# A two-layer hybrid decoder: a plain last eighth of the last layer's MLP, the loads of the DRAM sum on GpSimd's queue, decay two heads at a time, and mixing norms as columns

## The chip, the cores and the metric

The kernel runs on one core of one Trainium2 chip. The core has TensorE (PE; its weight loads appear as PEld), VectorE (DVE), ScalarE (ACT), GpSimd (POOL) and SyncE (SP), which only issues DMAs here. Time is the device time of one execution in microseconds; the median of three runs before is 1518.3 us (1516.29 to 1518.72).

## The reference

T is 512 tokens, D is 1024, and there are two layers. What the change touches is set off below by comments.

```python
def hybrid_layer(x, g_mix, w_in, sinks, w_a, w_b, w_out, g_mlp, w_up, w_down):
    h = rmsnorm(x, g_mix)                    # the mixing norm
    aq, ak, av, rq, rk, rv, rg, ga, gb = jnp.split(h @ w_in, SPLIT_POINTS, axis=-1)
    ya = sliding_window_sink_attention(rope_half(aq), rope_half(ak), av, sinks) @ w_a
    r = chunkwise_retention(retention_rotation(rq), retention_rotation(rk) * 128**-0.5, rv)   # four heads, decay
    r = r * lax.rsqrt(jnp.mean(r * r, axis=-1, keepdims=True) + EPS)
    yb = (r * jax.nn.silu(rg)) @ w_b
    x = x + (jax.nn.sigmoid(ga) * ya + jax.nn.sigmoid(gb) * yb) @ w_out
    h2 = rmsnorm(x, g_mlp)
    return x + jnp.square(jax.nn.relu(h2 @ w_up)) @ w_down      # D_FF = 4096, in eight blocks of 512
# after both layers: rmsnorm(x, g_final)
```

## The kernel before

**Products.** Activations lie transposed: 128 features on the partitions, tokens along a row. Every float32 operand is cut into a high part (ACT copies it to float32r, L301, L354) and a low part (DVE subtracts, L302, L355), and each product is three matmuls, high by high, high by low and low by high (`products`, L347 to L349).

**Weights.** They come in units of 128 x 1024 float32 (512 KB), in the order that `unit_order` lists. `load_until` issues their loads on SP's queue into five `raw` buffers, up to `AHEAD` = 4 units ahead of the split; `split_until` cuts them `SPLIT` = 3 units ahead of the matmuls. The instructions are put in order on each engine by a planner that simulates the program; an engine then executes its queue strictly in that order, and so does SP with its DMAs. The planner takes a DMA early if its buffer is free.

**The mixing stage.** `group` multiplies the first four units into four PSUM banks; its argument `meanwhile` names work to do after unit 0, 1, 2 or 3. In layer 1 this is `carried` after unit 0 (it finishes the x of layer 0, scales it, and sums its squares in `acc`, L477), `prepare` after unit 2 and `stats` after unit 3. `Rms.prepare` splits `acc`; `Rms.finish`, called by `stats`, multiplies both parts by a matrix of ones (L489), which gives every partition the sum over features of each token, and takes the root (ACT, L490) and the reciprocal (DVE, L491) of the 128 x 512 result. `scaled_tables` multiplies the rotary tables by it, and `rotate` (L537 to L543) uses those tables to empty the banks of k and q. `rstd_columns` turns the same norm into one column for each block of 128 tokens (four transposes). Attention and `retention` run as generators in the background of the products.

**Decay.** `Head.scores` multiplies the scores of a retention head by its decay tile `dm` (L851). Each head loads its own 256 KB tile (L841) on SP's queue into the one buffer of tag `acc`, which the squares of the norm use too. Tiles of 128 x 1024 float32 (`big`) share six buffers: the rotary tables, the gates `z` and `gb`, attention's `whole`, retention's `rr`, and in the MLP `z`, `xg`, `sums` and `y`.

**The MLP.** It runs over eight blocks e of 512 hidden features. `pair` multiplies twice 256 hidden features and `down` multiplies 512 by 1024 of `w_down`, both by a scheme with seven products of half-size blocks in place of eight; `Forms` makes the sums of activations that it wants. The sums of weights are made in DRAM by DMAs on POOL's queue, which add as they write (`sum_steps`, L213 to L227), five steps for every nine calls of `pace` in the mixing stage; `load_part` and `load_block` read them back. In a `down`, a unit feeds 2 x 2 x 3 = 12 matmuls of 512 columns, and seven units make 84. For e below 7 the results are added into a DRAM tensor `y` by adding DMAs on POOL's queue (`Adding`, L1219). For e = 7, `Ending` loads the four 512 KB parts of `y` back on SP's queue (L1233) when the block begins, and DVE adds the last results to them (L1248). In layer 1 they land in `x`, and the final norm and the output follow for each block of 128 tokens (L1256 to L1268).

Of the kernel before, what the change touches and what calls it, by code (L numbers as in the profile page):

```python
# [55 lines left out]
def unit_order():  # L56
# [9 lines left out]
    for e in range(N_BLOCK):  # L66
        if e == 0:
            order += [("w_up", u) for u in range(4)]
        else:
            order += [("pair", 2 * e - 2 + i, part) for i in range(2) for part in range(4)]  # L70
        order += [("block", e, part) for part in range(7)]
# [40 lines left out]
def decoder(ctx, tc, xT, x_first, w_in, w_a, w_b, w_out, w_up, w_pair, w_down, tables, decay, band, g_last, out):  # L112
# [45 lines left out]
    order = [(layer, *u) for layer in range(DEPTH) for u in unit_order()]  # L158
# [17 lines left out]
    def load_until(n):  # L176
        while state["loaded"] < min(n, len(order)):
# [6 lines left out]
            else:  # L184
                raws[i] = raw_tile()
                for at in halves(i):
                    queue = nc.scalar if i == 0 and at.start == 0 else nc.sync
                    queue.dma_start(raws[i][:, at], weights[name][layer, j][:, at])
# [11 lines left out]
    sums_last = [dram.tile([P, 2 * UNIT], F32, name=f"sums_last{l}") for l in range(DEPTH)]  # L200

    def sum_steps(layer):

        jobs = []
        for e in range(N_BLOCK):
            if e:
                jobs += [(sums_up[layer][n], w_pair[layer, n], UNIT) for n in (2 * e - 2, 2 * e - 1)]
            jobs.append((sums_down[layer][e], w_down[layer, e], 2 * UNIT))
        last = None
        for job in jobs + [None]:  # L210
# [6 lines left out]
            last = job  # L217
            yield
        e = N_BLOCK - 1
        both = sums_last[layer].rearrange("p (a n) -> p a n", a=2)  # L220
        first = sums_down[layer][e][:, UNIT:].unsqueeze(1).broadcast_to([P, 2, UNIT])
        r11, r12 = (w_down[layer, e][:, a * UNIT : (a + 1) * UNIT] for a in (0, 3))
        nc.gpsimd.dma_start(both, r11.unsqueeze(1).broadcast_to([P, 2, UNIT]))
        yield
        nc.gpsimd.dma_start(both, first, accum_op=ALU.add)
        yield
        nc.gpsimd.dma_start(both[:, 1, :], r12, accum_op=ALU.add)  # L227
# [4 lines left out]
    def pace(src):  # L232

        pace_count[0] += 1
        if steps and pace_count[0] * 5 // 9 > (pace_count[0] - 1) * 5 // 9:
# [27 lines left out]
    def load_block(i):  # L263
        layer, _, e, part = order[i]
        if part in (2, 4) and e < N_BLOCK - 1:
            return
        raws[i] = raw = raw_tile()
        source, at = {
            0: (w_down[layer, e], 0),
            1: (sums_down[layer][e], 1),  # L270
            2: (sums_last[layer], 0),
            3: (w_down[layer, e], 3),
            4: (sums_last[layer], 1),
# [210 lines left out]

    def inverse_rms(both, n, dest):
# [18 lines left out]
    class Rms:  # L504
# [15 lines left out]
    def layer_body(layer):  # L520
# [36 lines left out]
        rcol = small.tile([P, NB], F32, tag="rcol", name="rcol", bufs=2)  # L557

# [7 lines left out]

        def stats_first():
            rms_mix.prepare()
            stats()

        def rstd_columns():

            ps = bank(ps_aux, "rcol")
            for b in range(NB):
                nc.tensor.transpose(ps[:, b * P : (b + 1) * P], rstd()[:, b * P : (b + 1) * P], ident)
            nc.scalar.activation(rcol, ps.rearrange("p (b q) -> p b q", q=P)[:, :, 0], AF.Copy)

# [40 lines left out]
        def put_q(c):  # L618
# [18 lines left out]
            {0: squares, 1: stats_first} if layer == 0 else {0: carried.pop(), 2: rms_mix.prepare, 3: stats},  # L637
# [144 lines left out]
        def values(pair):  # L782
# [48 lines left out]
        class Head:  # L831
# [62 lines left out]

        def retention(pair):
# [31 lines left out]
        rstd_columns()  # L927
# [5 lines left out]
        qk(1)  # L933

# [105 lines left out]
        def column_factors():  # L1040
            ps = bank(ps_aux, "ssq")
            acc = acc_of.pop(g_mlp)
            for b in range(NB):
# [457 lines left out]
```

## Time and profile before

| | before |
|---|---|
| median of three runs | 1518.3 us |
| the profiled execution's own time | 1520.31 us |
| its span, first to last instruction | 1518.4 us |
| PE busy | 1477.2 us (97%) |
| DVE busy | 1059.8 us (70%) |
| ACT busy | 945.6 us (62%) |
| POOL busy | 239.6 us (16%) |
| mean granted TensorE clock | 0.987 of full speed |
| moved by DMA | 292.55 MB, 193 GB/s |

A line of the timeline gives the start in us from the beginning of the span, the length in us, the engine, the line of the kernel, the operation, the tile written and the tiles read, and the shape; "[4.48 <-DVE s L851]" says that the engine was idle for 4.48 us before it and that an instruction of DVE on L851 ended the wait. SPq and ACTq are the queues on which those engines issue DMAs. A line of the stages gives a stretch, its length, the busy time and number of instructions of each engine, the granted PE clock (1.00 is full speed), the share of the 16 DMA engines' time and the rate in GB/s. A line of the chain of waits gives start, length and what the chain passed through.

### The profile page before, as it was taken

Reading aid. Unit: us, or ns where it says so; the run is one execution under the profiler, and the core shown is the slowest. Engines: PE = TensorE matmul, PEld = TensorE weight load, DVE = VectorE, ACT = ScalarE, POOL = GpSimd, SP = SyncE. Lnnn points to the kernel's source line nnn. Section 1 sums busy time; section 2 is a strip of 40 time slices with the busy share of each in tenths; the row PEclk is TensorE's granted clock in tenths of the full one; section 3 lists DMA queues with packets and bytes.
Section 4 is the critical chain, followed back from the end, with each engine's and each line's share of the span. In section 5 each row is a group of like instructions: output and inputs, shape, how many; then the busy total and the mean of one; then the engine's idle time right before and its main releaser. Section 6 shows DMA issues by size and latency. Waiting matters only on the chain.

```text
span 1518.4 us, 21303 instructions
## 1 busy us (share of the span) xinstructions
PE 1477.2 (97%) x7767; PEld 1271.5 (84%) x7767; DVE 1059.8 (70%) x1602; ACT 945.6 (62%) x1560; POOL 239.6 (16%) x337
## 2 busy tenths in 40 slices
PE   9999999899999999999999999999999999999986
PEld 7888888788889899998778888878888889899975
DVE  7877667564677777775987775667547677677757
ACT  7656454443568888886655563546325788888865
POOL 0001211010002222222001011110000122222220
PEclk9999999999999999999999999999999999999998
DMA  7655997566327888889747579975643388888893
GB/s 263 194 158 159 265 285 193 159 180 165 99 74 214 211 214 218 222 212 227 253 131 206 166 193 255 262 208 156 168 136 109 109 217 218 204 214 220 219 233 118
DMA packets 103481, 292.55 MB, mean 193 GB/s; under 512 B 11856, under 2 KB 11984, under 8 KB 99280
## 3 DMA queue, kind: packets, MB, share of 16 engines
q0 software_dynamic: 38656, 114.84, 36.3%
q1 hardware_dynamic: 64000, 175.04, 34.3%
q8 instruction: 61, 1.00, 0.3%
q10 hardware_dynamic: 720, 1.31, 0.2%
q14 instruction: 44, 0.36, 0.1%
HBM read 237.66 MB, written 118.49 MB: 235 GB/s over the span
## 4 chain that ended last, share of the span: by engine, by line
PE 72%; DMA 11%; issue 7%; DVE 5%; ACT 3%; POOL 1%; SPq 0%; DVEq 0%; ACTq 0%; POOLq 0%
PE mm L347 19%; PE mm L348 19%; PE mm L349 19%; DMA raw<-w_pair_in 3%; DMA raw<-w_down_in 2%; DMA y<-y 2%; DMA dm<-decay_in 2%; DVE lo L302 2%; PE rv L347 2%; DMA y<-eu 2%; PE rv L349 2%; PE rv L348 2%; ACT hi L301 1%; PE b L347 1%; PE b L348 1%
## 5 line engine op out<-in xcount | busy, mean ns | idle before, releaser
L301 ACT ACTIVATE hi<-raw 128x1024 fp32r<-128x1024 f32 (+1 forms) x366 | 372.9, 1020 | 313.4 <-PE mm L348 192.0
L302 DVE TENSOR_TENSOR lo<-raw,hi 128x1024 fp32r<-128x1024 f32 (+1 forms) x367 | 427.9, 1170 | 188.2 <-ACT hi L301 184.1
L347 PE MATMUL mm<-xh,hi 128*128 128x512 f32 (+1 forms) x1008 | 360.0, 360 | 16.5 <-ACT eu L1129 11.6
L349 PE MATMUL mm<-xh,lo 128*128 128x512 f32 (+1 forms) x1008 | 357.3, 357 | 0.7 <-DVE lo L302 0.7
L348 PE MATMUL mm<-xl,hi 128*128 128x512 f32 (+1 forms) x1008 | 357.9, 357 | 0.0
L347 PE MATMUL mm<-r,hi 128*128 128x256 f32 (+1 forms) x736 | 239.1, 325 | 0.5 <-ACT mm L1127 0.5
L348 PE MATMUL mm<-r,hi 128*128 128x256 f32 (+1 forms) x736 | 239.3, 325 | 0.0
L349 PE MATMUL mm<-r,lo 128*128 128x256 f32 (+1 forms) x736 | 239.2, 325 | 0.0
L347 PEld LDWEIGHTS mm<-xh,hi 128*128 128x128 f32 x1008 | 192.4, 191 | 45.2 <-ACT eu L1129 13.5
L349 PEld LDWEIGHTS mm<-xh,lo 128*128 128x128 f32 x1008 | 192.0, 190 | 26.3 <-DVE lo L302 0.9
L348 PEld LDWEIGHTS mm<-xl,hi 128*128 128x128 f32 x1008 | 192.3, 191 | 25.6
L347 PEld LDWEIGHTS mm<-r,hi 128*128 128x128 f32 x736 | 140.5, 191 | 13.8 <-ACT mm L1127 0.7
L348 PEld LDWEIGHTS mm<-r,hi 128*128 128x128 f32 x736 | 140.4, 191 | 13.3
L349 PEld LDWEIGHTS mm<-r,lo 128*128 128x128 f32 x736 | 140.3, 191 | 11.3
L1219 POOL DMA_DIRECT2D y<-eu x56 | 47.3, 851 | 403.3 <-ACT eu L1217 399.2
L1219 POOL DMA_DIRECT2D y<-y x112 | 97.9, 1277 | 64.1 <-DMA y<-eu 19.9
L348 PE MATMUL mm<-lo,r 128*128 128x512 f32 x256 | 98.3, 393 | 0.0
L349 PE MATMUL mm<-hi,r 128*128 128x512 f32 x256 | 94.4, 390 | 0.0
L347 PE MATMUL mm<-hi,r 128*128 128x512 f32 x256 | 93.0, 396 | 0.2
L261 DVE TENSOR_TENSOR raw<-raw 128x512 f32<-128x512 f32 x56 | 38.5, 687 | 66.1 <-DMA raw<-sums_up 53.8
L347 PE MATMUL b<-hi,r 128*128 128x512 f32 x192 | 75.3, 392 | 1.9 <-DVE y L1248 1.4
L348 PE MATMUL b<-lo,r 128*128 128x512 f32 x192 | 74.9, 390 | 0.0
(255 smaller groups left out, 2341.1 us busy)
## 6 DMA issues: line engine op xcount, KB each, us to landing
raw<-w_in_in SPq DMA_DIRECT2D x89, 512.0 KB, 5.1
sums_down<-w_down_in POOLq DMA_DIRECT2D x32, 1024.0 KB, 11.3
y<-y POOLq DMA_DIRECT2D x120, 256.0 KB, 7.7
sums_up<-w_pair_in POOLq DMA_DIRECT2D x56, 512.0 KB, 10.5
raw<-w_down_in SPq DMA_DIRECT2D x48, 512.0 KB, 8.3
raw<-w_pair_in SPq DMA_DIRECT2D x84, 256.0 KB, 4.1
raw<-sums_down SPq DMA_DIRECT2D x32, 512.0 KB, 8.7
y<-eu POOLq DMA_DIRECT2D x58, 256.0 KB, 5.6
```

The lines of the kernel that those rows point to most:

```text
L261: nc.vector.tensor_tensor(raws[i][:, at], last[:, LEFT], last[:, RIGHT], ALU.add)
L301: nc.scalar.activation(hi[:, at], raw[:, at], AF.Copy)
L302: nc.vector.tensor_tensor(lo[:, at], raw[:, at], f32(hi[:, at]), ALU.subtract)
L347: nc.tensor.matmul(ps, ah, bh, start=start and i == 0, stop=False, **more)
L348: nc.tensor.matmul(ps, ah, bl, start=False, stop=False, **more)
L349: nc.tensor.matmul(ps, al, bh, start=False, stop=stop and i == n - 1, **more)
L1219: nc.gpsimd.dma_start(y[:, block, i * T : (i + 1) * T], t, **how)
```

## The change

1. **Plain last eighth.** In layer 1, block e = 7 multiplies `w_down` in the ordinary way: a new input `w_end` holds its 512 rows in four units of 128 x 1024 in place of the seven units of the block, and `down_plain` makes 4 units x 4 token blocks x 2 halves x 3 = 96 matmuls of 512 columns. Token blocks 0 and 1 are summed over the four units as these arrive, in four banks, and blocks 2 and 3 after them, a half at a time. The forms of this block, its DRAM sums and `sums_last` of layer 1 fall away.
2. **Loads of the DRAM sum.** The four loads of `y` in `Ending` are issued on POOL's queue.
3. **Decay.** `load_decay` loads the tiles of two heads in one DMA of 512 KB into a `big` buffer: the first pair's before `values(0)`, the second pair's after the scores of head 1.
4. **Mixing norms.** `prepare` sums `acc` over features with four matmuls by a single column of ones (`token_sums`), takes root and reciprocal of the 128 x 4 result, spreads it on the diagonals of four 128 x 128 blocks, and splits that tile; `finish` multiplies by the ones as before and copies the bank. The columns serve the retention values, and `rstd_columns` is gone. In layer 0, `prepare` follows unit 1 and `stats` unit 2; layer 1 keeps 2 and 3.
5. **Pace.** A step of the DRAM sums is taken at each second call of `pace`; a layer has 48 calls, 24 steps in layer 0 after the change (26 before) and 22 in layer 1.

```diff
@@ unit_order(layer)
+        if layer == DEPTH - 1 and e == N_BLOCK - 1:
+            order += [("w_end", k) for k in range(4)]
+        else:
+            order += [("block", e, part) for part in range(7)]
@@ load_until
+                    source = w_end[j] if name == "w_end" else weights[name][layer, j]
+                    queue.dma_start(raws[i][:, at], source[:, at])
@@ sum_steps
+            if e < whole:
+                jobs.append((sums_down[layer][e], w_down[layer, e], 2 * UNIT))
...
+        if whole == N_BLOCK:
...
+            nc.gpsimd.dma_start(sums_last, r11.unsqueeze(1).broadcast_to([P, 2, UNIT]))
             yield
+            nc.gpsimd.dma_start(sums_last, s1.unsqueeze(1).broadcast_to([P, 2, UNIT]), accum_op=ALU.add)
+            nc.gpsimd.dma_start(sums_last[:, 1, :], r12, accum_op=ALU.add)
@@ pace
-        if steps and pace_count[0] * 5 // 9 > (pace_count[0] - 1) * 5 // 9:
+        if steps and pace_count[0] % 2 == 0:
@@
+    def token_sums(acc):
+        ps = bank(ps_aux, "ssq")
+        for b in range(NB):
+            nc.tensor.matmul(ps[:, b : b + 1], acc[:, b * P : (b + 1) * P], f32(ones)[:, 0:1], start=True, stop=True)
+        return ps
@@ class Rms
         def prepare(self):
-            self.parts = sum_parts(acc_of.pop(self.which))
+            acc = acc_of.pop(self.which)
+            ps = token_sums(acc)
+            self.columns = small.tile([P, NB], F32, tag="rcol", name="rcol", bufs=2)
+            nc.scalar.activation(self.columns, ps[:, :NB], AF.Sqrt, bias=eps, scale=1.0 / D)
+            nc.vector.reciprocal(self.columns, self.columns)
+            wide = temp("wide")
+            nc.vector.tensor_tensor(
+                wide.rearrange("p (b q) -> p b q", q=P),
+                ident.unsqueeze(1).broadcast_to([P, NB, P]),
+                self.columns.unsqueeze(2).broadcast_to([P, NB, P]),
+                ALU.mult,
+            )
+            self.parts = sum_parts(wide)
         def finish(self):
             self.value = tmp.tile([P, T], F32, tag="rstd", name="rstd", bufs=1)
-            inverse_rms(self.parts, D, self.value)
+            ps = bank(ps_aux, "ssq")
+            for i, part in enumerate(self.parts):
+                nc.tensor.matmul(ps, ones, part, start=i == 0, stop=i == 1)
+            nc.scalar.activation(self.value, ps, AF.Copy)
@@ layer_body
-            {0: squares, 1: stats_first} if layer == 0 else {0: carried.pop(), 2: rms_mix.prepare, 3: stats},
+            {0: squares, 1: rms_mix.prepare, 2: stats} if layer == 0 else {0: carried.pop(), 2: rms_mix.prepare, 3: stats},
...
-                split(view(hi), view(lo), ps, rcol[:, b : b + 1])
+                split(view(hi), view(lo), ps, rms_mix.columns[:, b : b + 1])
@@ Head.scores
-                    self.dm = tmp.tile([P, T], F32, tag="acc", name="dm", bufs=1)
-                    nc.sync.dma_start(self.dm, decay[:, h, :])
+                    self.dm = decays[h // 2][:, h % 2, :]
@@
+        def load_decay(pair):
+            decays[pair] = big("dm")
+            nc.sync.dma_start(decays[pair], decay[:, 2 * pair : 2 * pair + 2, :])
@@ retention
                     head.scores(js)
+                    if pair == 0 and head is two[1] and js[0]:
+                        load_decay(1)
                     yield
@@
-        rstd_columns()
...
         qk(1)
+        load_decay(0)
         values(0)
@@ the MLP
+        def first_plain(z):
+            nc.scalar.activation(z, z, AF.Square)
+            split(*u_forms.tiles[0][0], z.rearrange("p a (b t) -> p (a b) t", t=H))
...
+        def down_plain(into):
+            sums.free()
...
+            units = []
+            early = [[bank(pool, "mm") for pool in (ps_mm, ps_aux)] for _ in range(2)]
+            for k in range(4):
+                units.append(unit("w_end", layer))
+                for m in range(2):
+                    for half in range(2):
+                        add(early[m][half], m, half, k)
+            for m in range(2):
+                for half in range(2):
+                    into.put(half, m // 2, m % 2, early[m][half], 1)
+            for m in range(2, NB):
+                for half in range(2):
+                    ps = bank(ps_mm, "mm")
+                    for k in range(4):
+                        add(ps, m, half, k)
+                    into.put(half, m // 2, m % 2, ps, 1)
@@ class Ending
-                    nc.sync.dma_start(two, y[:, 2 * j : 2 * j + 2, i * T : (i + 1) * T])
+                    nc.gpsimd.dma_start(two, y[:, 2 * j : 2 * j + 2, i * T : (i + 1) * T])
...
-                if last or i == 0:
+                if i == 0:
@@
-            down(e, into)
+            if last and e == N_BLOCK - 1:
+                down_plain(into)
+            else:
+                down(e, into)
```

More of the change, by code (lines that the diff above doesn't have):

```diff
@@ L111, in decoder @@
 @with_exitstack
-def decoder(ctx, tc, xT, x_first, w_in, w_a, w_b, w_out, w_up, w_pair, w_down, tables, decay, band, g_last, out):
+def decoder(ctx, tc, xT, x_first, w_in, w_a, w_b, w_out, w_up, w_pair, w_down, w_end, tables, decay, band, g_last, out):
     nc = tc.nc
@@ L155, in decoder @@
     spill = dram.tile([P, KD, T], F32, name="spill")
-    order = [(layer, *u) for layer in range(DEPTH) for u in unit_order()]
+    order = [(layer, *u) for layer in range(DEPTH) for u in unit_order(layer)]
     raws, parts = {}, {}
@@ L199, in decoder @@
     sums_down = [dram.tile([N_BLOCK, P, 2 * UNIT], F32, name=f"sums_down{l}") for l in range(DEPTH)]
-    sums_last = [dram.tile([P, 2 * UNIT], F32, name=f"sums_last{l}") for l in range(DEPTH)]
+    sums_last = dram.tile([P, 2, UNIT], F32, name="sums_last")
     def sum_steps(layer):
+        whole = N_BLOCK if layer < DEPTH - 1 else N_BLOCK - 1
         jobs = []
@@ L267, in load_block @@
         raws[i] = raw = raw_tile()
+        if part in (2, 4):
+            nc.sync.dma_start(raw, sums_last[:, part // 2 - 1, :])
+            return
         source, at = {
@@ L1040, in column_factors @@
         def column_factors():
-            ps = bank(ps_aux, "ssq")
-            acc = acc_of.pop(g_mlp)
-            for b in range(NB):
-                nc.tensor.matmul(ps[:, b : b + 1], acc[:, b * P : (b + 1) * P], f32(ones)[:, 0:1], start=True, stop=True)
+            ps = token_sums(acc_of.pop(g_mlp))
             nc.vector.tensor_scalar(factor, ps[:, :NB], 1.0 / D, EPS, ALU.mult, ALU.add)
@@ L1092, in second_rest @@
         def second_rest(z):
+            if not kept:
+                return
             kept.pop()
@@ L1332, in layer_body @@
             else:
+                plain = last and e == N_BLOCK - 1
                 into = Ending() if e == N_BLOCK - 1 else Adding(e)
```

46 lines of the change are left out of this document (22 added, 24 removed).

## The prediction

> **What bounds the kernel now.** I read the page's busy times first, then PE's timeline for its idle stretches, then the stages around each.
>
> ```profile
> PE 1477.2 (97%) x7767; PEld 1271.5 (84%) x7767; DVE 1059.8 (70%) x1602; ACT 945.6 (62%) x1560; POOL 239.6 (16%) x337
> ```
>
> PE is the bound: what the change can win is matmuls, PE's idle time, time at a lower clock, and the tail. The timeline of PE has five long idle stretches; the sixth row is a short one, for comparison.
>
> ```profile
> 275.37 0.47 PE L347 MATMUL ret<-r,r 128*128 128x128 f32 x1 [4.48 <-DVE s L851]
> ...
> 722.12 0.58 PE L347 MATMUL mm<-xh,hi 128*128 128x256 f32 x1 [3.56 <-ACT eu L1129]
> ...
> 784.24 0.47 PE L347 MATMUL mm<-xh,hi 128*128 128x512 f32 x1 [3.56 <-DVE rot L541]
> ...
> 1025.67 0.48 PE L347 MATMUL ret<-r,r 128*128 128x128 f32 x1 [3.96 <-DVE s L851]
> ...
> 1479.87 0.58 PE L347 MATMUL mm<-xh,hi 128*128 128x256 f32 x1 [5.29 <-ACT eu L1129]
> ```
>
> ```profile
> 746.50 0.47 PE L347 MATMUL b<-hi,r 128*128 128x512 f32 x1 [1.40 <-DVE y L1248]
> ```
>
> The stages right behind the five (PE alone: length, busy time, granted clock, DMA) show a second price of each.
>
> ```profile
> 275.37:280.27 4.90, 4.90 (x17) 0.50 0.33 65
> ...
> 722.11:727.41 5.30, 5.29 (x21) 0.50 1.04 406
> ...
> 784.24:788.85 4.61, 4.61 (x13) 0.63 0.35 117
> ...
> 1025.67:1031.20 5.53, 5.53 (x18) 0.50 0.17 47
> ...
> 1479.87:1485.17 5.30, 5.30 (x23) 0.50 0.97 381
> ```
>
> ```profile
> 745.00:750.00 5.00, 3.60 (x20) 3.03 (x20) 5.00 (x8) 0.53 (x1) 0.00 (x0) 1.00 0.62 205
> ```
>
> After each long stretch PE runs at half clock for a while; after the 1.40 us one the clock stays 1.00. What is lost there is length times (1 - clock): 2.45, 2.65, 1.71, 2.77, 2.65. With the idle time the five cost 6.93, 6.21, 5.27, 6.73 and 7.94 us: 33.1 us, and four parts of the change each touch one or two of them.
>
> **Decay (275 and 1025).** The chain of waits goes through a load of `dm`, and DVE's row shows the wait.
>
> ```profile
> 258.56 16.03 DMA dm<-decay_in
> ```
>
> ```profile
> 274.62 1.48 DVE L851 TENSOR_TENSOR s<-ret,dm 128x512 f32<-128x512 f32 x3 [10.54 <-DMA dm<-decay_in]
> ```
>
> One buffer serves all heads, so the load of the pair's second head can start only when the first has been multiplied, and it lands 16.03 us after its issue, among DRAM sums. The change loads two heads at once, the second pair's right behind the scores of the first, with two `qk` and a `values` (8 units, each 24 matmuls) between. A matmul of 512 columns starts every 0.227 us (three in 0.68):
>
> ```profile
> 237.68 0.39 PE L347 MATMUL rv<-hi,xh 128*128 128x512 f32 x1
> ...
> 238.36 0.39 PE L347 MATMUL rv<-hi,xh 128*128 128x512 f32 x1
> ```
>
> so 8 x 24 x 0.227 = 43.6 us cover a load that took 16. Both stretches go: -13.7 us. Without that cover nothing is won. The first pair's tile is asked for before `values(0)`, with that and the four units of `w_a` (43.6 us again) before it is wanted. On SP's queue nothing new waits as long as one of the six `big` buffers is free: live when the first is taken are the tables, two `z`, and at most the last `whole`; with both decay tiles that is six, and before the second `rr` the first decay tile is free.
>
> **Mixing norms as columns (784).** This is the start of layer 1: the third, fourth and fifth bank wait for `rotate`, that for tables, those for the norm.
>
> ```profile
> 766.82 0.68 DVE L477 TENSOR_TENSOR acc<-acc,sq 128x512 f32<-128x512 f32 x1
> ```
>
> ```profile
> 774.63 0.39 PE L489 MATMUL ssq<-sh,ones 128*128 128x512 f32 x1
> ```
>
> ```profile
> 775.73 1.28 ACT L490 ACT_TABLE_LOAD   x1
> 777.02 0.69 ACT L490 ACTIVATE rstd<-ssq,x 128x512 f32<-128x512 f32 x1
> ```
>
> ```profile
> 777.75 3.35 DVE L491 RECIPROCAL rstd<-rstd 128x512 f32<-128x512 f32 x1 [0.78 <-ACT rstd L490]
> ```
>
> ```profile
> 1509.23 0.21 DVE L1262 RECIPROCAL sq<-sq 128x1 f32<-128x1 f32 x2
> ```
>
> ```profile
> 428.15 0.79 PE ssq L1044 x8
> ```
>
> The squares are done at 767.50. Unit 3 has 24 matmuls ahead of 774.63, so unit 2 ends at 769.2; there the four column sums go (0.79 us, as the MLP's same sums take). Then table load and root 1.97 at most, reciprocal of 4 columns about 0.1, diagonal 0.68 (the 128x512 row of DVE), high and low part 0.63 and 0.68: 774.1. The two products with ones stay at 774.6 and take 0.45, the copy out 0.63: 775.7, and up to 2.3 if a unit's split on ACT and one on DVE come first. Now the norm is there at 781.10 and PE goes on 3.14 later; then it would be 778.8 to 781.1. PE runs out of work at 780.68 (784.24 less 3.56). So at most 0.4 is left, and I take 0.3: -5.0. The extra cost on PE is at most 0.79 per layer less four transposes that go; I take 0.8 for both layers. In layer 0 there is no long idle stretch to win.
>
> **Loads of the DRAM sum (722 and 1479).** SP's queue, ACT's timeline, and the stage of the idle time:
>
> ```profile
> 1424.25 0.33 SPq L255 DMA_DIRECT2D raw<-w_pair_in  x1
> ```
>
> ```profile
> 1463.80 3.58 SPq L1233 DMA_DIRECT2D x<-y  x2
> 1467.47 0.46 SPq L255 DMA_DIRECT2D raw<-w_pair_in  x1
> ```
>
> ```profile
> 705.63 3.53 SPq L1233 DMA_DIRECT2D late<-y  x2
> 709.26 0.42 SPq L255 DMA_DIRECT2D raw<-w_pair_in  x1
> ```
>
> ```profile
> 1430.84 0.63 ACT L301 ACTIVATE hi<-raw 128x512 fp32r<-128x512 f32 x1 [0.84 <-PE mm L348]
> ```
>
> ```profile
> 1476.61 0.63 ACT L301 ACTIVATE hi<-raw 128x512 fp32r<-128x512 f32 x1 [7.22 <-DMA raw<-w_pair_in]
> ...
> 1479.45 0.36 ACT L1129 ACTIVATE eu<-mm 128x256 f32<-128x256 f32 x1
> ```
>
> ```profile
> 1474.57:1479.87 5.30, 0.01 (x2) 0.86 1.03 412
> ```
>
> SP stands at the loads of `y` until the adding DMAs of e = 6 have landed, and the last part of a pair waits behind them; ACT waits 7.22 us to cut it, and behind that on ACT stands the evacuation (L1129) that PE wants. On POOL's queue the same loads stand behind the same adding DMAs, and nothing else of e = 7 is behind them but two adding DMAs of layer 0 that need them anyway. The part leaves 3.67 us sooner in layer 1 and 3.63 in layer 0. In layer 0 that covers the 3.56; I leave 0.3: -5.9. In layer 1 the part would be cut at 1472.94 and L1129 end at 1476.14, 1.6 us after PE ran dry (1474.58), and behind 1.6 us the clock does not fall. But it also took 9.14 us from issue to ACT, and 6.59 in the block before, where no loads of `y` ran along: then nothing is left. Between 0 and 1.6 I take 0.8: -7.1. The other end is the 16.03 us of the decay load: the part would then come 3.2 us later than now, and nothing would be won.
>
> By the Trainium skill (DMA: Bandwidth & Descriptors, Queues, rings and completion order) each DMA engine takes turns between the queues it has work for, so the weights would get their turn while the loads of `y` wait in the other queue. By that rule the left-over 0.8 goes too and the sum below is 31.0 in place of 30.2. That the stage's engines are full (1.03) is why I do not take it.
>
> **Plain last eighth.** 96 matmuls in place of 84: 12 x 0.227 = +2.7 us. The weights fall from seven units to four. The last hidden part is wanted only with the fourth unit, 36 matmuls (8.2 us) into the stage, which hides its square and split. The tail:
>
> ```profile
> 1506.24 0.39 PE L349 MATMUL b<-hi,r 128*128 128x512 f32 x1
> ```
>
> ```profile
> 1506.71 0.74 DVE L1248 SCALAR_TENSOR_TENSOR x<-b,columns,x 128x512 f32<-128x512 f32 x1
> 1507.37 1.28 DVE L1257 TENSOR_TENSOR x<-x,late 128x512 f32<-128x512 f32 x2
> ```
>
> ```profile
> 1513.26 0.35 ACTq L1268 DMA_DIRECT2D y_out<-x  x1
> ```
>
> Now two token blocks end together: from the last matmul's start to the end are 12.2 us, 5.1 of them from the last output's issue. Then only one ends last: matmul 0.39, add 0.74, square 0.63 (as ACT's 128x512 copy), root and reciprocal of one column some 0.5, scaling 0.7 (as ACT's 0.69), and 5.1, so 8.1. DVE needs some 3.8 us per token block (two adds, two gains of 0.64, the scaling) against 24 x 0.227 = 5.4 on PE, but starts with two blocks at once, so up to 1.3 behind. Between -4.1 and 0 (DVE as late as now) I take -3.0.
>
> **Pace.** The DRAM sums end one call of `pace` later. POOL is idle for 96.59 us before its first work in the MLP, which hides that:
>
> ```profile
> 449.74 0.60 POOL L1219 DMA_DIRECT2D y<-eu  x1 [96.59 <-ACT eu L1217]
> ```
>
> **The sum.** -13.7 - 5.0 - 5.9 - 7.1 - 3.0 + 2.7 + 0.8, and +1.0 for a new short wait (the 1.40 row is the measure): -30.2 us. The profiled execution, 1520.31 us with a span of 1518.4, would be 1490.1; it lay 2.0 over the median of the runs, 1518.3, which would be **1488**.
>
> **The rivals.**
> *The loads collide all the same.* The DMA engines are full at 722 and 1479 and the bytes of `y` stay. If the weights take 16 us as the decay load did, both stretches stay: +13.0, 1501. For it the shares of 1.03 and 1.04; against it that the block before, as full of adding DMAs, delivers in 6.6.
> *The decay tile comes late after all,* since SP is in order and the planner may put the load behind a full raw buffer: +13.7, 1502. The 43.6 us speak against it.
> *The column sums make PE wait.* They stand in PE's queue 1.7 us behind the last square. If the squares slip by more, PE stands where it did not: the 5.0 are lost and some 2 more, 1495.
> *Slower: the decay tiles hold `big` buffers.* If a seventh tile is live, SP stands at `load_decay(0)` until the rotary tables are last read, with all weights behind it.
>
> ```profile
> 225.91 0.68 DVE L542 TENSOR_TENSOR rot<-rot,tab 128x512 f32<-128x512 f32 x1
> ```
>
> ```profile
> L851 DVE TENSOR_TENSOR s<-ret,dm x32: 280/484/692, 192.4 to 1029.2; 128x512 f32<-128x512 f32 x8, 128x384 f32<-128x384 f32 x8, 128x256 f32<-128x256 f32 x8, 128x128 f32<-128x128 f32 x8
> ```
>
> Decay is first wanted at 192.4, so 34 us per layer: 1488 + 13.7 + 68 = 1570. It makes the kernel slower once over 8.3 us per layer reach PE. My count of six live tiles speaks against it; it has nothing to spare.
>
> **How the numbers follow.** The forecast has 0.61, with a range of its own of 1482 (every stretch gone, 33.1 + 4.1 - 2.7 and the rest at nothing, is 1484; DVE and DMA relief 2 more) to 1494 (the plan of the queues, made anew, costs 5). The collision has 0.13, the late decay 0.08, the column sums 0.09, the buffers 0.09, of which 0.02 lie near no change. The range 1481 to 1503 leaves out the buffers and the worst of the others. What a measurement of this kernel can tell from no change is about 0.2%, 3 us. Faster 0.91, same 0.02, slower 0.07.
>
> **What would show it.** Right: no idle row on PE over 2 us with L851, L541 or L1129 behind it; granted clock 1.00 throughout until the tail; the part's load on SP at e = 7 issued some 2 us behind the one before it; no load of `dm` in the chain of waits; twelve more matmuls of 512 columns at the end, and under 10 us from the last of them to the end. Wrong: a wait of SP at `load_decay`, a wait of PE on the columns, or idle PE in the last block with the weights of `w_end` behind it.

## The result, and the profile after

The changed kernel takes 1500.81 us (median of four runs, 1498.23 to 1502.41) against 1518.51 (1516.29 to 1522.29) for the kernel before on the same chip: a ratio of 0.9879 with a 95% interval of 0.9855 to 0.9904, so 17.7 us less. A second series (the run called again) gives 0.9875 (0.9855 to 0.9896). The forecast was 30.2 us less. The profiled execution took 1501.42 us with a span of 1499.7; its mean granted clock is 0.997 (before 0.987).

The page's busy times of the changed kernel:

```profile
PE 1471.8 (98%) x7787; PEld 1265.7 (84%) x7787; DVE 1044.3 (70%) x1589; ACT 940.9 (63%) x1551; POOL 239.7 (16%) x334
```

PE's timeline, the rows that answer to the long idle stretches of before (idle time and its releaser in brackets):

```profile
712.62 0.39 PE L354 MATMUL mm<-xh,hi 128*128 128x256 f32 x1 [1.80 <-ACT eu L1154]
...
773.67 0.80 PE L354 MATMUL mm<-xh,hi 128*128 128x512 f32 x1 [2.83 <-DVE rot L570]
...
1464.01 0.39 PE L354 MATMUL mm<-xh,hi 128*128 128x256 f32 x1 [2.02 <-ACT eu L1154]
```

Three of the five are still there, shorter. Both at the decay are gone; the row of the groups for that multiplication shows no wait for a load any more:

```profile
L863 DVE TENSOR_TENSOR s<-ret,dm 128x512 f32<-128x512 f32 (+3 forms) x32 | 14.6, 483 | 2.1 <-PE ret L356 1.9
```

The stages behind the three (length, PE busy, granted clock, DMA share, GB/s), to be read against the 0.50 to 0.63 of before:

```profile
712.62:717.62 5.00, 5.00 (x33) 1.00 1.04 377
773.67:778.67 5.00, 5.00 (x16) 0.72 0.34 108
...
1464.00:1469.00 5.00, 4.99 (x33) 1.00 0.94 280
```

Two of them run at full clock; at the start of layer 1 the half clock is still there for part of the time.

What came in its place is in the blocks of the MLP. The groups of instructions, PE alone, over blocks one to six of one layer (after the second bar: idle time in all, then by what ended it). First before, layer 0 and layer 1, then the changed kernel in the same order:

```profile
L347 PE MATMUL mm<-xh,hi 128*128 128x256 f32 x157 | 45.1, 287 | 1.0 <-ACT eu L1129 0.9
L347 PE MATMUL mm<-xh,hi 128*128 128x256 f32 x157 | 45.0, 287 | 1.8 <-ACT eu L1129 1.8
```

```profile
L354 PE MATMUL mm<-xh,hi 128*128 128x256 f32 x149 | 42.9, 288 | 0.3 <-ACT eu L1154 0.3
L354 PE MATMUL mm<-xh,hi 128*128 128x256 f32 x151 | 43.9, 291 | 5.3 <-ACT eu L1154 5.3
```

In layer 1 the idle time behind the evacuation of a pair went from 1.8 to 5.3 us.

The tail: the last matmul, DVE's last addition, and the last output's issue.

```profile
1490.03 0.39 PE L356 MATMUL mm<-hi,r 128*128 128x512 f32 x1
```

```profile
1491.96 0.73 DVE L1307 SCALAR_TENSOR_TENSOR x<-mm,columns,x 128x512 f32<-128x512 f32 x1
```

```profile
1495.66 0.34 ACTq L1327 DMA_DIRECT2D y_out<-x  x1
```

From the last matmul's start to the end of the span are 9.7 us; before it was 12.2.

### The profile page after: what moved, and what is told of

Read it like the earlier page. It is cut to its first block, busy times and chain, and to the rows that moved or that the text cites. A ratio compares the mean times of both kernels' runs of the same rounds, so it can differ in the third digit from the quotient of the medians.

```text
span 1499.7 us, 21303 instructions
## 1 busy us (share of the span) xinstructions
PE 1471.8 (98%) x7787; PEld 1265.7 (84%) x7787; DVE 1044.3 (70%) x1589; ACT 940.9 (63%) x1551; POOL 239.7 (16%) x334
## 4 chain that ended last, share of the span: by engine, by line
PE 87%; DMA 6%; ACT 3%; DVE 2%; issue 2%; DVEq 0%; ACTq 0%
PE mm L354 23%; PE mm L355 23%; PE mm L356 23%; DMA raw<-w_down_in 3%; DMA raw<-w_pair_in 2%; PE rv L354 2%; PE rv L356 2%; PE rv L355 2%; PE b L354 2%; PE b L355 2%; PE b L356 2%; DVE lo L309 1%; PE score L705 1%; ACT hi L308 1%; PE pT L670 1%
## 5 line engine op out<-in xcount | busy, mean ns | idle before, releaser
L354 PEld LDWEIGHTS mm<-xh,hi 128*128 128x128 f32 x1008 | 190.7, 189 | 44.2 <-ACT eu L1154 12.5
L354 PEld LDWEIGHTS mm<-r,hi 128*128 128x128 f32 x736 | 139.8, 190 | 13.7 <-ACT mm L1152 0.7
L355 PEld LDWEIGHTS mm<-r,hi 128*128 128x128 f32 x736 | 139.8, 190 | 13.1
L355 PE MATMUL mm<-lo,r 128*128 128x512 f32 x272 | 104.2, 392 | 0.0
L356 PE MATMUL mm<-hi,r 128*128 128x512 f32 x272 | 100.7, 390 | 0.0
L354 PE MATMUL mm<-hi,r 128*128 128x512 f32 x272 | 97.8, 393 | 0.2
L354 PE MATMUL b<-hi,r 128*128 128x512 f32 x180 | 70.5, 392 | 1.6 <-DVE y L1307 1.6
L355 PE MATMUL b<-lo,r 128*128 128x512 f32 x180 | 70.3, 390 | 0.0
```

The lines of the kernel that those rows point to most:

```text
L354: nc.tensor.matmul(ps, ah, bh, start=start and i == 0, stop=False, **more)
L355: nc.tensor.matmul(ps, ah, bl, start=False, stop=False, **more)
L356: nc.tensor.matmul(ps, al, bh, start=False, stop=stop and i == n - 1, **more)
```

## The experiments

All are told against the kernel before, run beside them on the same chip (its medians there were 1519.74, 1518.79, 1518.39 and 1518.62 us); "us to before" is the difference of the medians. Against the changed kernel, the measure is the -17.6 of `again` for the runs beside it (u_decay_pace, u_pace, e_norm), and the mean of -17.7 and -17.6 for the others. The intervals are 4 to 7 us wide, so a difference of 1 or 2 us between two rows can't be told from nothing.

| run | what it is | median, us | us to before | ratio (95%) |
|---|---|---|---|---|
| u_norms | changed kernel, norms undone | 1503.24 | -16.5 | 0.989 (0.987 to 0.991) |
| u_loads | loads of the DRAM sum undone | 1511.81 | -7.9 | 0.9948 (0.993 to 0.9966) |
| u_decay | decay undone | 1507.17 | -12.6 | 0.9914 (0.9894 to 0.9934) |
| u_plain | last eighth undone | 1502.63 | -17.1 | 0.9886 (0.9867 to 0.9906) |
| u_decay_pace | decay and pace undone | 1514.33 | -4.5 | 0.9965 (0.9947 to 0.9983) |
| u_pace | pace undone | 1499.93 | -18.9 | 0.9873 (0.9855 to 0.9891) |
| again | changed kernel | 1501.22 | -17.6 | 0.9875 (0.9855 to 0.9896) |
| b_decay | kernel before, decay changed | 1505.15 | -13.2 | 0.9917 (0.9905 to 0.9929) |
| e_norm | PE's order at the norms | 1496.85 | -21.9 | 0.9856 (0.9836 to 0.9875) |
| e_norm_eu | and ACT's order in the pairs | 1509.23 | -9.2 | 0.9942 (0.993 to 0.9954) |
| e_place | new weights and DRAM tiles placed elsewhere | 1499.61 | -18.8 | 0.9879 (0.9866 to 0.9892) |
| e_norm_spare | e_norm, DRAM tiles placed elsewhere | 1496.24 | -22.4 | 0.9855 (0.9832 to 0.9878) |

**One part undone at a time.**

u_norms:

```diff
         def prepare(self):
-            ps = token_sums(acc)
...
-            self.parts = sum_parts(wide)
+            self.parts = sum_parts(acc_of.pop(self.which))
```

> Only the norms go back to the old way (squares cut, two products with ones, root and reciprocal of 128x512, four transposes for the columns); the rest is the changed kernel. Theory (from the two profiles): the part is worth about 1.0 us and not the 5.0 forecast, because the planner put the column sums and the two products with ones 3 to 4.5 us later in PE's queue than their inputs are there: 1501 + 1 = 1502 us, and the idle time of PE at the start of layer 1 goes from 2.83 back to about 3.6 us. Rival: the norms are worth the 5.0 and something else took 4 of it: 1506 us, with the idle time at the start of layer 1 back at 3.6 us and the other short waits 3 to 4 us less.

1.1 us more than the changed kernel, and PE's idle time at the start of layer 1 back at 3.51 us (PE's timeline):

```profile
775.91 0.77 PE L354 MATMUL mm<-xh,hi 128*128 128x512 f32 x1 [3.51 <-DVE rot L555]
```

The five us behind it have a granted clock of 0.50, against 0.72 in the changed kernel. By the medians the part as it stands is worth about 1 us, by these two rows nearly 2; the intervals tell it neither from nothing nor from 4. The theory is the nearer one; why it is so little is e_norm's question.

u_loads:

```diff
-                    nc.gpsimd.dma_start(two, y[:, 2 * j : 2 * j + 2, i * T : (i + 1) * T])
+                    nc.sync.dma_start(two, y[:, 2 * j : 2 * j + 2, i * T : (i + 1) * T])
```

> Only the four loads of the DRAM sum go back to SP's queue, in both layers. Theory: they are what the part of the pair waits for; PE's idle time in the last block goes from 1.80 back to about 3.6 us in layer 0 and from 2.02 to about 5.3 us in layer 1, each with half clock behind it again, +4.0 and +5.6 = +9.6 us: about 1510 us. Rival: what is left in the changed kernel (2.02 us) comes from DMA engines that are full either way, and most of the gain came with the smaller last block: under +5 us, at most 1506.

9.7 us more. Both stretches are back, in PE's timeline:

```profile
715.30 0.57 PE L354 MATMUL mm<-xh,hi 128*128 128x256 f32 x1 [4.32 <-ACT eu L1154]
...
1470.99 0.58 PE L354 MATMUL mm<-xh,hi 128*128 128x256 f32 x1 [5.28 <-ACT eu L1154]
```

So SP's standing was the cause. Full DMA engines were not: they are as full in the changed kernel (1.04 behind 712.62), where both waits are less than half as long.

u_plain:

```diff
-            if last and e == N_BLOCK - 1:
-                down_plain(into)
-            else:
-                down(e, into)
+            down(e, into)
```

with seven units, the DRAM sums of this block and a tile `sums_last` for each layer again.

> Only the last eighth of layer 1 goes back to seven products, with its sums in DRAM (one pair of them for each layer, as before). Theory: the twelve matmuls (+2.7) and the shorter tail (-2.6) cancel, so 1501 us within 2, the tail from PE's last start back at about 12 us; the short waits of PE in the first six blocks of layer 1 (9.1 us of lost time in the changed kernel, 4.7 before) stay as they are. Rival: these waits come with this part (where the new weights and the sums lie in DRAM), then they fall back to 4.7 and the time is about 1497 us.

0.5 us more than the changed kernel, which can't be told from nothing. Both theories have a share: in layer 1 the idle time fell to what it was before (the group of PE over blocks one to six of layer 1),

```profile
L354 PE MATMUL mm<-xh,hi 128*128 128x256 f32 x151 | 43.5, 288 | 1.9 <-ACT eu L1154 1.8
```

but a wait of 1.80 us came up in the last block and the tail is 12.9 us again:

```profile
1484.54 0.47 PE L354 MATMUL b<-hi,r 128*128 128x512 f32 x1 [1.80 <-ACT junk L1315]
```

**Decay and pace.** u_decay loads each head's tile by itself, into the one buffer of `acc`:

```diff
-                    self.dm = decays[h // 2][:, h % 2, :]
+                    self.dm = tmp.tile([P, T], F32, tag="acc", name="dm", bufs=1)
+                    nc.sync.dma_start(self.dm, decay[:, h, :])
```

> Only the decay goes back to one head at a time, from one buffer. Theory: the two waits of DVE for the load of the second head are back, with PE idle for about 4.5 and 4.0 us and at half clock behind it: +13.8 us, about 1514.5 us. Rival: the pace of the DRAM sums, which also changed, took the load's latency down by itself: under +5 us.

It cost 5.1 us and not 13.8: nearly the rival's figure. The wait is back, but short (DVE's timeline, the chain of waits and PE's timeline of u_decay):

```profile
268.72 1.16 DVE L864 TENSOR_TENSOR s<-ret,dm 128x512 f32<-128x512 f32 x2 [5.13 <-DMA dm<-decay_in]
```

```profile
259.53 9.16 DMA dm<-decay_in
```

```profile
269.46 0.33 PE L354 MATMUL ret<-r,r 128*128 128x128 f32 x1 [1.01 <-DVE s L864]
...
1012.60 0.33 PE L354 MATMUL ret<-r,r 128*128 128x128 f32 x1 [1.59 <-DVE s L864]
```

The load of the pair's second head takes 9.2 us where it took 16.0, and PE stands 1.0 and 1.6 us where it stood 4.5 and 4.0 (and 0.85 us for a first head, at 210.50). The buffer and the moment of the issue are those of before (258.56 there, 259.53 here); what differs in POOL's timelines is the sums beside it (issued at 259.23, 263.30 and 263.82 there, at 264.30 and 265.11 here). That was tried next.

u_decay_pace is u_decay with

```diff
-        if steps and pace_count[0] % 2 == 0:
+        if steps and pace_count[0] * 5 // 9 > (pace_count[0] - 1) * 5 // 9:
```

and u_pace is the changed kernel with that line alone.

> The decay goes back to one head at a time and the pace of the DRAM sums back to five steps in nine calls (the changed kernel: one in two); the rest is the changed kernel. Theory: undoing the decay alone cost only about 5 us, since with the slower pace fewer sums run beside the load of the second head (it landed after 9.2 us and not 16.0); with both undone the load takes 13 us or more again and PE stands about 4 us at both places: 1513 to 1515 us against 1507 with the decay alone undone. Rival: the pace has nothing to do with it and the latency is the plan's chance: within 2 us of 1507.

> Only the pace of the DRAM sums goes back to five steps in nine calls. Theory: with two heads of decay loaded 43 us ahead, what a load takes beside the sums no longer matters: no difference, 1501 us within 2, and no idle time of PE behind the multiplication by the decay. Rival: the pace is worth something by itself, other loads come late beside denser sums: 1504 us or more.

u_decay_pace cost 13.1 us, u_pace nothing (1.3 us less, inside its interval). The load is slow again in the chain of waits of u_decay_pace:

```profile
261.11 14.27 DMA dm<-decay_in
```

Its eight runs spread from 1508 to 1518 us, and the profiled one is the shortest (1507.97), so that profile, with 2.71 us of idle time at the first place and 1.03 at the second, does not itemize the 13.1. Of the other seven only span and clock are known: the clock is 0.990 to 0.994 against the 0.996 of the profiled one, which points to more time at half clock; the waits behind it were not seen.

b_decay is the kernel before with `load_decay` alone.

> The kernel before with the decay alone changed (two heads at a time, the second pair's load behind the first pair's scores). Theory: both waits for the second head go although the pace of the DRAM sums is the old one, which takes the 13.8 us of the two places out of the profile of before: 1505 us, no idle time of PE behind the multiplication by the decay. Rival: beside the denser sums the loads of decay or of weights come late elsewhere: 1510 us or more.

1505.15 us, 13.2 less than before, and no idle time of PE at the decay. So the two ways to end these stalls overlap. Two heads at a time end them alone, at either pace; the slower pace alone takes 8 of the 13 us.

The loads did not stand where the text of the change puts them. SP's queue in the changed kernel has both pairs' loads of layer 0 together, the second long before the scores of head 1:

```profile
144.33 0.94 SPq L911 DMA_DIRECT2D dm<-decay_in  x2
```

DVE multiplies by the first tile from 173.21 and by the second pair's from 250.61, so the cover is 28.9 and over 100 us, and the four loads of the two layers landed 12.8 to 17.7 us after their issue. They are no faster than the 16.03 us of before, but nothing waits for them.

**The order at the norms.** e_norm changes no instruction, only PE's order at the start of layer 1: `last_sum` holds the last of the four column sums while unit 3 of the group is issued, and the last product with ones when the next chunk is:

```diff
+    def behind(wanted):
+        return tc.issue_after(last_sum[0].ins) if wanted else nullcontext()
@@ group
+            with behind(u == 3 and meanwhile and layer > 0):
...
@@ token_sums
+            last_sum[0] = nc.tensor.matmul(ps[:, b : b + 1], acc[:, b * P : (b + 1) * P], f32(ones)[:, 0:1], start=True, stop=True)
@@ Rms.finish
+                last_sum[0] = nc.tensor.matmul(ps, ones, part, start=i == 0, stop=i == 1)
@@ layer_body
+        with behind(layer > 0):
+            chunk("w_in", layer, xs, put_q(2))
```

> The changed kernel, with the fourth unit's matmuls at the start of layer 1 ordered behind the four column sums, and the next chunk's behind the two products with ones. Theory: the columns and the diagonal are fast enough, only PE's order was late; the products then stand some 24 matmuls behind the sums, near 764 us in place of 769, the tables come 4 us sooner, PE's 2.83 us of idle time and the half clock behind it go: about 1497 us (-4). Rival: the chain of root, reciprocal, diagonal and split stands in ACT's and DVE's queues behind other work all the same, and PE now waits at the products instead: idle time over 2 us stays, 1501 us or more.

21.9 us less than before, 4.4 less than the changed kernel beside it. The two intervals overlap; e_norm_spare below, with the same order, has 22.4. PE's timeline of the changed kernel first, then of e_norm:

```profile
761.12 0.95 PE L496 MATMUL ssq<-ones,acc 128*128 128x1 f32 x8
...
768.87 0.39 PE L543 MATMUL ssq<-sh,ones 128*128 128x512 f32 x1
...
769.55 0.39 PE L543 MATMUL ssq<-sl,ones 128*128 128x512 f32 x1
```

```profile
760.72 0.94 PE L503 MATMUL ssq<-ones,acc 128*128 128x1 f32 x8
...
767.11 0.39 PE L551 MATMUL ssq<-sh,ones 128*128 128x512 f32 x1
767.34 0.39 PE L551 MATMUL ssq<-sl,ones 128*128 128x512 f32 x1
```

The two profiles are shifted, so they are read by their distances. e_norm's products stand 6.4 us behind the sums and not 7.8, and its sums stand at the end of unit 2, twelve matmuls (2.7 us) sooner in PE's order. The stages from there (ten us each, the changed kernel first):

```profile
767.00:777.00 10.00, 7.17 (x26) 0.83 0.34 107
```

```profile
766.00:776.00 10.00, 10.00 (x46) 1.00 0.17 55
```

No idle time and full clock. The rival (a wait at the products) did not come. ACT, DVE and SP change some places too, between 762 and 808 us; outside of that the order on them and on POOL is the same in both profiles.

**ACT's order in the pairs.** In the pairs, PE waits for an evacuation, `eu<-mm`, that stands in ACT's queue behind the split of a later weight unit. e_norm_eu orders that split behind it:

```diff
-            nc.scalar.activation(eu[:, :H], e, AF.Copy)
-            part = unit("pair", layer)
+            ev = nc.scalar.activation(eu[:, :H], e, AF.Copy)
+            with tc.issue_after(ev.ins):
+                part = unit("pair", layer)
```

> e_norm, with the split of the weight unit that the pair's second part asks for ordered behind the evacuation eu<-mm of the same pair on ScalarE. Theory: what makes PE stand in the blocks is the order in ACT's queue (the evacuation stands behind a split whose weights land late), not the late weights themselves, since PE has three units in hand: the idle times behind that evacuation (3.8 us in layer 1 and 1.8 us in layer 0 of e_norm) fall under 1.5 us together, 4 to 5 us less than e_norm's 1497: 1492 to 1493 us. Rival: PE needs the late unit soon after in any case, and stands at the next evacuation or at the unit itself: the idle time stays, 1496 us or more.

A miss: 1509.23 us, about 12 over e_norm. The rival is the nearer one: PE stands again soon after, though at neither of the places that it names. The groups of e_norm_eu and of e_norm for the first matmuls of `down` (idle time over the whole span):

```profile
L355 PE MATMUL b<-hi,r 128*128 128x512 f32 x180 | 72.6, 403 | 12.9 <-ACT r L362 12.9
```

```profile
L355 PE MATMUL b<-hi,r 128*128 128x512 f32 x180 | 70.5, 392 | 1.4 <-DVE y L1316 1.4
```

The evacuation is nearly on time now (0.1 and 1.0 us of idle time behind it in blocks one to six of the two layers), and the split of the hidden part (`r`, L362) is late in nearly every block: 11.5 us more. In these blocks, what was pushed back on ACT pushed the next thing back.

**Where the data lie.** e_place is the changed kernel with `w_end` last among the inputs and an unused DRAM tile in the place of the second `sums_last`; e_norm_spare is e_norm with that tile alone:

```diff
+    spare_last = dram.tile([P, 2, UNIT], F32, name="spare_last")
     sums_last = dram.tile([P, 2, UNIT], F32, name="sums_last")
```

> The changed kernel once more, unchanged. For the short waits of PE in the blocks of layer 1 (idle times over 0.25 us behind the evacuation of the pair, blocks one to seven: 7.3 us in the changed kernel's profile, 1.6 before, 4.5, 3.4, 3.6 and 1.7 with the norms, decay, loads and last eighth undone, the old loads' own wait left out). Theory: they are the chance of one execution's transfers, and come out between 2 and 6 us here; then the 2.02 us in the last block is chance too, and under 0.5 us here. Rival: they belong to this program, 7 us again and 2 us in the last block. Time 1501 us in either case.

> The changed kernel with the new weights last among the inputs and a second, unused tile beside the sums of the last block, so that the DRAM tiles behind them lie as before. Theory: the short waits in the blocks of layer 1 (4.3 us in the repeat of the changed kernel, 1.6 before and with the last eighth undone) come from where the data lie in DRAM; they fall to about 2 us and the time by 2 to 3, to 1498.5. Rival: placement is not it; 4 us of waits and 1501 us again.

> e_norm with the unused tile beside the sums of the last block alone; the new weights stay where the changed kernel has them. PE's time lost in blocks one to six was 3.5 us in layer 1 before, 4.2 to 4.5 in the two kernels without the new weights, 6.6 to 9.2 in the eight with them, and 5.0 with the new weights moved last and this tile (where layer 0 rose from 0.9 to 2.9 up to 5.0). Theory: where the kernel's own DRAM tiles lie decides; layer 1 falls to 5 us or less, layer 0 stays under 3, and the time is 2 to 3 us under e_norm's, 1494 to 1495. Rival: where the inputs lie decides; layer 1 stays over 6.5 us and the time at 1497.

The idle time behind the evacuation in blocks one to six, as in the rows above: with the changed kernel's layout it is 3.1 to 5.3 us in layer 1 in eight profiles (the changed kernel, again, u_norms, u_loads, u_decay, u_decay_pace, u_pace, e_norm) and 0 to 1.2 in layer 0. With the spare tile, e_norm_spare's groups, layer 0 and then layer 1, are

```profile
L356 PE MATMUL mm<-xh,hi 128*128 128x256 f32 x151 | 43.5, 288 | 3.0 <-ACT eu L1164 2.8
L356 PE MATMUL mm<-xh,hi 128*128 128x256 f32 x148 | 42.5, 287 | 1.0 <-ACT eu L1164 0.9
```

and e_place's 2.3 and 2.5. An unused tile adds no instruction, and the order on ACT, DVE, SP and POOL is the same in the profiles of e_norm and e_norm_spare; the tile moves what lies behind it in DRAM, and the waits go from layer 1 to layer 0. So the theory's first half holds (layer 1 falls), its second does not (layer 0 rises), and the time stays (1496.24 against 1496.85). e_place's 1.2 us under `again` can't be told from nothing either. Of again, the blocks' part went to the rival (4.3 us, not the chance of one execution), and the last block's to the theory: no idle time there, and 0 to 0.7 us in the other profiles with the loads on POOL. The 2.02 us was chance. That the waits of layer 1 go with where the new weights and tiles lie agrees with all these profiles: u_plain, with 1.8, has in these blocks the same order on ACT, DVE and SP as the changed kernel, and ran beside u_norms, u_loads and u_decay, which have 3.2 to 4.9. But it rests on one profile of each kernel, and the two with the spare tile come from other chips than seven of the eight (that of the changed kernel's own profile is not on record), so chance and the chip are not wholly ruled out. How addresses would slow the transfers, and why before and u_plain have it low in both layers (0.9 and 1.8, 0.7 and 1.8), stays open.

## Why the prediction was right, and where not

The sign and the range (1481 to 1503) hold 1500.8; the forecast of 1488 and its own range of 1482 to 1494 do not. The stages that it named are the ones that changed, but 12.5 us of the 30.2 are missing by the medians, and 11.5 between the two profiles (spans of 1518.4 and 1499.7). Of these 11.5, 3.9 are at the norms, 2.7 at the loads, 1.8 in blocks one to six (3.5 more in layer 1, 0.7 less in layer 0, 1.0 put down) and 0.5 in the tail. Some 2 are matmul time: summed over stretches of five us, PE's idle time went from 41.2 to 27.9 us and what it lost to the clock from 12.4 to 1.2, while the time of its matmuls at full clock rose by 5.7 where 3.5 were forecast.

**Decay: right.** -13.7 forecast, -13.2 with b_decay. That a cover ends the wait is shown: u_pace, with the denser sums, has none there. The 43.6 us were not what ran, since SP took both loads early and the first had 28.9 us; against the 12.8 to 17.7 that the loads took, that was enough. It also means that both decay tiles were held at once from the start, with no `big` buffer to spare by the prediction's count, and SP did not stand at `load_decay`.

**Pace: right in time, wrong in reach.** It was costed at nothing by its cover in the MLP, and u_pace shows nothing. But it also thins the sums beside the decay loads; beside u_decay it is worth 8 us (13.1 less 5.1). The prediction looked only at the sums' own end.

**Norms: the failed step, 3.9 us.** Of the idle time and half clock here 0.3 us was to be left; the profile has 2.83 us idle and, at 0.72 over five us, 1.4 lost to the clock. (The -5.0, or -4.2 with the 0.8 for the column sums, is not to be set against u_norms alone, whose 1.1 is within the noise.) The durations were right (root 0.26, reciprocal 0.18, diagonal 0.69, in ACT's and DVE's timelines of the changed kernel):

```profile
762.10 0.26 ACT L528 ACTIVATE rcol<-ssq,x 128x4 f32<-128x4 f32 x1 [1.32 <-PE ssq L496]
```

```profile
755.22 1.41 DVE L484 TENSOR_TENSOR acc<-acc,sq 128x512 f32<-128x512 f32 x2
...
762.40 0.18 DVE L529 RECIPROCAL rcol<-rcol 128x4 f32<-128x4 f32 x1 [1.66 <-ACT rcol L528]
762.83 0.69 DVE L531 TENSOR_TENSOR wide<-ident,rcol 128x512 f32<-128x512 f32 x1 [0.25 <-DVE rcol L529]
764.81 0.69 DVE L362 TENSOR_TENSOR sl<-wide,sh 128x512 fp32r<-128x512 f32 x1 [1.28 <-ACT sh L361]
```

"There the four column sums go" is what failed, and "the two products with ones stay". The squares were done at 756.63, the sums stood at 761.12, twelve matmuls into unit 3; the parts were there at 765.50, the products stood at 768.87, 18 matmuls into the next chunk. So they came 2.0 us before PE ran out of work (770.84); in the kernel before it was 6.1 (774.63 and 780.68), and the prediction kept that. PE's order is the planner's; why it gave a shorter chain later places is not shown. e_norm, which changes places alone, brings 4.4 us by the medians and ends the wait, so the rest of the 5.0 was there to have. The rival "column sums make PE wait" had the place and the wrong mechanism: PE did not wait at them, it came to them late.

**Loads of the DRAM sum: mechanism right, 3.3 us over-sized.** -13.0 for both, 9.7 measured; 1.80 us for 0.3 and 2.02 for 0.8 are 2.7 of the difference in the profile. In layer 0, 0.3 us was to be left and 1.80 is, in all ten profiles with the loads on POOL and ACT's order as it is. What sets it is no load but an order; ACT's timeline in layer 0:

```profile
710.02 1.06 ACT L308 ACTIVATE hi<-raw 128x1024 fp32r<-128x1024 f32 x1 [2.45 <-PE mm L355]
...
711.24 1.05 ACT L308 ACTIVATE hi<-raw 128x1024 fp32r<-128x1024 f32 x1
712.19 0.37 ACT L1154 ACTIVATE eu<-mm 128x256 f32<-128x256 f32 x1
```

Two splits of units stand ahead of the evacuation, the first of them waiting for PE to give a buffer back. In e_norm_eu, which orders a split behind it, 0.51 us is left here. The prediction followed the part of the pair to its split and took the way from there to L1154 as it had been. In layer 1 the profile has 2.02 left, and there it is a unit's load:

```profile
1458.96 0.63 ACT L308 ACTIVATE hi<-raw 128x512 fp32r<-128x512 f32 x1 [2.16 <-DMA raw<-w_pair_in]
...
1462.63 1.06 ACT L308 ACTIVATE hi<-raw 128x1024 fp32r<-128x1024 f32 x1 [1.68 <-DMA raw<-w_end_in]
1463.59 0.36 ACT L1154 ACTIVATE eu<-mm 128x256 f32<-128x256 f32 x1
```

with the loads issued (SP's queue) at

```profile
1451.16 0.33 SPq L261 DMA_DIRECT2D raw<-w_pair_in  x1
1451.76 5.86 SPq L192 DMA_DIRECT2D raw<-w_end_in  x4
```

The pair's part took 7.8 us to its split, between the 6.6 and 9.1 of the bounds; the first unit of `w_end` took 10.9. That is the third of the signs that the prediction named for being wrong (idle PE in the last block with `w_end` behind it). The other profiles have 0 to 0.7 us here, around the 0.8 taken. The Trainium skill (DMA: Bandwidth & Descriptors, Queues, rings and completion order) has the engines take turns between queues, by which the left-over goes; that agrees with those profiles and not with this one; no run here shows the turns themselves.

**Plain eighth and tail: right within the noise.** The twelve matmuls were forecast at +2.7 us and not measured by themselves; the tail at -3.0 measured -2.5, with DVE's last addition starting 1.9 us behind the last matmul's start. Undone, the part is worth 0.5 us for a forecast of 0.3, less than a measurement tells.

**New short waits: the other failed step.** +1.0 was put down after one row of 1.40; layer 1 alone has 3.5 us more in its blocks. The place was not foreseen at all: in blocks one to six of layer 1 the order on ACT, DVE, SP and POOL is the same in the profiles before and after, and what the change moves there is where the data lie.

**The rivals.** The collision gave 1501, which is the time by chance and not the cause: u_loads shows that the loads' move brought 9.7 us. No tile of decay was late, and SP did not stand at `load_decay`.

**What does not add up.** Undone singly, norms, loads and eighth are worth 1.1, 9.7 and 0.5 us, and decay and pace together 13.1: 24.4, against 17.7 for the whole. Where the 6.7 us between them lie was not seen.

## What to carry to other kernels

A saving on a chain that crosses engines counts only from the places that its instructions get in each queue: read off where they will stand, and if a planner writes the order, tie it down where the profile shows inputs ready before their turn (4.4 us by the medians here, for no instruction more; the same on ACT, in the pairs, cost 12). Undo parts singly and together before adding their gains: two parts that end the same wait, as the decay tiles and the pace do, are not worth their sum. And after any change of DRAM tiles or inputs look at the transfers of stages that were not touched.

## What the runs showed of the hardware

The granted clock falls behind much shorter waits than the prediction allowed ("behind 1.6 us the clock does not fall"), but not each time. The same wait of 1.80 us in layer 0 is followed by full clock in five of the ten profiles that have it (the changed kernel at 712.62, above) and by 0.66 over five us in the other five (e_norm and u_plain among them), and the same 2.83 us at the start of layer 1 by 0.72 in the changed kernel and 1.00 in again. PE's row of e_norm and the stages, of e_norm and then of again:

```profile
713.77 0.48 PE L355 MATMUL mm<-xh,hi 128*128 128x256 f32 x1 [1.80 <-ACT eu L1163]
```

```profile
713.77:718.77 5.00, 5.00 (x25) 0.66 1.04 370
```

```profile
774.25:779.25 5.00, 5.00 (x22) 1.00 0.35 108
```

Taken singly, the us in the middle of e_norm's stage have 0.50, so 0.66 over 5 us is half clock for 3.4 us, 1.7 us lost. The Trainium skill (TensorE: Matmul & The Clock Gate, Part 1: The HAM clock gate) speaks of a free-running window of about 3.4 us, which would fit a fall that comes at one time and not at another. But it has the clock fall after a whole idle window, and the page's section "Why this matters for your kernels" warns only of idle gaps over about 3 us; the 1.80 us of these rows are less, and in five profiles the clock fell.
